# Layer B of a two-layer streaming encoder: the weight tile that was scanned for its scale is kept and split, and is not loaded a second time

## The chip, the cores and the metric

The kernel runs on one core of a Trainium2 chip. The metric is the time of one execution on the device, in microseconds (us). Runs are single executions; the median of several stands for a kernel. One further execution is recorded by the hardware profiler, and everything that is read from a trace comes from that one.

The engines are named as the profile does: PE (TensorE matmuls) with PEld (its weight loads), DVE (VectorE), ACT (ScalarE), POOL (GpSimd), SP (SyncE, which issues all DMAs here, in order).

## What is computed

Two attention layers over 2048 prompt tokens and 64 sample tokens, model width 1024, 16 heads of 64, in chunks of 64 frames. Each layer is

```
h = rms_norm(x, g);  q, k, v, gate = split(h @ w_in)
q, k = rms_norm per head;  o = softmax(q k' / 8 + bias) v
y = x + (o * silu(gate)) @ w_out
```

Layer A has 2 key/value heads, a learned sink per head and a T5 bias over the own chunk and 2 earlier ones. Layer B, where the change lies, has 16 key/value heads and a clipped relative bias over the own chunk and 8 earlier ones. The sample tokens attend to a cache (128 rows in layer A, 256 in layer B) and to themselves. The outputs are y for both, the newest keys and values of the prompt, and the rolled caches. Inputs and outputs are float32.

## The kernel before

**Precision.** Every large product is made from two parts of each operand, a high and a low one. In layer B the parts are float16, so weights have to be brought into its range: for each of the eight head pairs (hp) the kernel finds the largest absolute weight, times the norm's gain, and takes a power of two from it. `scan` (172) does this: it loads one of eight 128x512 pieces of the pair's input weights, and DVE reduces it to one maximum per partition (175). After eight pieces, `input_top` (231) takes the gain in and the maximum over the pieces; `input_across` (236) turns the column with a PE transpose (207) and works out the power of two with some ten tiny DVE passes; `input_scales` (243) spreads three numbers over all partitions with a PE matmul (222) and scales the gains (227).

**Splitting.** `load_weights` (454) loads the same pieces again for use, into a ring of 12 tiles called `wl` (470), and `split` makes the float16 parts: ACT the high one (498), DVE the low one (501). They go into another ring of 12, `wh`; eight belong to the pair in work, so at most four can be made early. `emit` (517) loads the first three pieces and queues splits; each split loads the next piece.

**Order of the work.** PE's order is written by hand. `Filler` (923) holds a list of projection jobs, one for each head pair and unit of tokens: u0 to u6, the sample unit (64 tokens), u7, then the next pair. PE alternates between attention of one unit (`pipeline`, 1717) and pieces of the projection jobs, which run about two units ahead. When a job starts, `step` (933) loads the next job's activations and, where a job a few places ahead opens a new head pair, calls its `weights` early: before, two jobs ahead with four splits (`early` = 2), and at one job ahead with the rest. The splits go into `Background` (389), a queue with costs, from which `share` (446) takes a few after each score block; in layer B at most one weight split each time. Work taken from it is ordered behind the last score pass on its engine (`anchor`, 407, and `behind`, 300), without a wait between engines. The other engines' order is made by a scheduler that moves an instruction forward where its operands are ready by its own estimate of times.

**The scans' places.** `scale_work(hp, u, e)` (271) runs after each projected tile (unit u, half e; at = 2u + e). Before, it loads one piece of the next pair's weights at each of at = 0 to 7, into the ring `wraw` of three tiles (or `scan`, of one), reduces it two tiles later, takes the maximum at at = 9, and appends `input_across` at 10 and `input_scales` at 12 to a list, `chain`. The attention loop runs one entry of that list after the fourth head of a unit (1775). Pieces 64 to 83, scanned at at = 11 to 13, belong to the output weights and the cached values.

**Attention in layer B.** `queries` (1406) transposes q and k of a unit, and ACT copies the high parts (1431, 1432); DVE makes the low ones (1443, 1447); two small DMAs copy q to the other half of the partitions (1436). At unit 1 it also loads the cache of the pair, `load_cache` (881), whose keys go into `KSA` and `KSB` (869, 870). `scores` (1459) runs the matmuls (1492, 1493; 1478 for the sample) into one of two PSUM banks `sb`; DVE adds the bias and takes the row's minimum (1496, 1501), ACT exponentiates (1505) and casts (1544), POOL subtracts for the low part (1545), a transposing DMA turns both (1553), and PE multiplies with the values (1650). For the sample, `sample_outputs` (1604) adds two parts on DVE (1614) and multiplies with the gate on POOL (1615); `sample_turned` (1617) transposes the result on PE (900).

Of the kernel before, what the change touches and what calls it, by code (L numbers as in the profile page):

```python
# [17 lines left out]
P = 128  # L18
# [10 lines left out]
HD = 64  # L29
# [24 lines left out]
TURNED = (0, 1)  # L54

@with_exitstack
def hybrid_encoder_kernel(
# [105 lines left out]
    scanned, pending = [], []  # L163

# [7 lines left out]
    def scan(i=None, keep=0):  # L172
# [71 lines left out]
    def input_scales(h):  # L244
        everywhere(h, row[:, 20:23])

# [24 lines left out]
    def scale_work(hp, u, e):  # L271
        at = 2 * u + e
        if hp < 7:
            if at < 8:
                scan(8 * (hp + 1) + at, 1)
            elif at == 8:
                scan(None, 1)
            elif at == 9:
                scan()
                input_top(hp + 1)  # L280
            elif at == 10:
                held["chain"].append(lambda: input_across(hp + 1))
            elif at == 12:
# [170 lines left out]
    def load_weights(g, *specs, scale=None):  # L454
# [7 lines left out]

        spare = 3 if len(specs) > 1 else 0
# [417 lines left out]
    def load_cache(ktsrc, vsrc, C, both):  # L881
# [41 lines left out]
    class Filler:  # L923
# [4 lines left out]
        def add(self, prefetch, weights, gen, early=3):  # L928
# [4 lines left out]
        def step(self):  # L933
            if self.gen is None:
# [35 lines left out]
    def layer_a():  # L970
# [4 lines left out]
        def add_unit(qd, place, unit):  # L975
# [120 lines left out]
            filler.add(prefetch, weights if place == 0 else None, first if qd == 0 and u == 0 else gen, 3 * (qd > 1))  # L1096
# [230 lines left out]
    def layer_b():  # L1327
# [4 lines left out]
        def add_unit(hp, unit):  # L1332
# [67 lines left out]
            filler.add(prefetch, weights if u == 0 else None, gen, 2)  # L1400
# [5 lines left out]
        def queries(it):  # L1406
# [6 lines left out]
            if u == 1:  # L1413
                load_cache(ckt_b[it.hp], cv_b[it.hp], CB, True)
# [15 lines left out]
            for hh, rows in enumerate(halves):  # L1430
                nc.scalar.activation(q1[hh][rows], qt[hh], AF.Identity, scale=gq[rows])
                nc.scalar.activation(kd[hh][rows], kt[hh], AF.Identity, scale=gk[rows])

            def copies():
                for hh, rows in enumerate(halves):
                    held["copy"] = load(wide(q1[hh][halves[1 - hh]]), wide(q1[hh][rows])).ins

# [166 lines left out]
        def sample_outputs(it):  # L1604
# [10 lines left out]
            nc.gpsimd.tensor_tensor(o, it.G[:, 0:HD], o, op=ALU.mult)  # L1615
# [399 lines left out]
```

## Time and profile before

| | |
|---|---|
| median of 3 runs | 2146.34 us (2141.74 to 2146.76) |
| profiled execution, its own time | 2147.27 us |
| span of its trace | 2145.5 us, mean granted clock 0.992 |
| instructions | 40906 |
| busy: PE, DVE, ACT, POOL | 95%, 70%, 67%, 54% of the span |
| DMA traffic of the kernel's queue | 402.35 MB, 69.7% of 16 DMA engines' span |
| layer B's input weights, second load (476) | 64 transfers of 256 KB |
| the same, load for the scan (184) | 56 transfers of 256 KB (and 8 more for the first pair, into `scan`) |

How to read it: "busy" is the share of the span in which an engine had an instruction running. Matmuls overlap, so PE's busy time counts the length of each, while its pace is set by how far apart they start. A line such as "PE sb L1492 <- DVE nm L1496: 11.5, 8, 1.9" in a list of waits says that line 1492 on PE, which works on the tile `sb`, stood idle for 11.5 us in 8 waits, the longest 1.9, and that an instruction of line 1496 on DVE, which wrote `nm`, ended them. In a timeline the columns are start, duration, engine, line, operation, output and inputs, and in brackets the idle time before and what ended it.

### The profile page before, as it was taken

The page shows a single profiled execution, that of the slowest core. Times are in us where ns is not written, and L with a number is a line of the kernel's source. Part 1 is how long each engine was busy: PE and PEld are TensorE (multiplying, and loading weights), DVE is VectorE, ACT ScalarE, POOL GpSimd, SP SyncE. Part 2 cuts the span into 40 slices and gives each one's busy share as a digit, 9 for nine tenths or more (in the row PEclk, how much of TensorE's full clock was granted, in tenths as well). Part 3 has the DMA queues.
Part 4 walks back from the last instruction along what each step waited for, and adds up shares of the span by engine and source line. Part 5 has one row for each costly group of instructions (what it writes and reads, how often), then busy time and mean ns, then how long its engine had stood idle before and what let it go on. Part 6 is the DMA issues. An engine that isn't in the chain of part 4 may idle for free.

```text
span 2145.5 us, 40906 instructions
## 1 busy us (share of the span) xinstructions
PE 2046.2 (95%) x12951; PEld 1467.4 (68%) x12951; DVE 1504.9 (70%) x4049; ACT 1428.7 (67%) x3610; POOL 1148.6 (54%) x1621
## 2 busy tenths in 40 slices
PE   7999999999999999888999999999999999898999
PEld 6887788778888999555555555555555555456887
DVE  6768778767767554677777777777867778577642
ACT  6878877767777333466667676777867768577420
POOL 5555544434445445774366676666766667566000
PEclk9999999999999999999999999999999999999999
DMA  8856545756544676744478799797887979668763
GB/s 277 269 168 209 176 155 191 211 168 212 163 149 133 211 220 182 243 149 156 136 173 205 186 194 224 169 229 177 194 213 175 241 156 202 153 144 193 228 198 116
DMA packets 512120, 404.96 MB, mean 189 GB/s; under 512 B 303696, under 2 KB 449376, under 8 KB 511872
## 3 DMA queue, kind: packets, MB, share of 16 engines
q1 hardware_dynamic: 511904, 402.35, 69.7%
q8 instruction: 102, 1.67, 0.3%
q14 instruction: 114, 0.93, 0.1%
HBM read 257.59 MB, written 73.43 MB: 154 GB/s over the span
## 4 chain that ended last, share of the span: by engine, by line
PE 62%; DVE 12%; ACT 8%; DMA 6%; issue 6%; POOL 4%; SPq 1%; ACTq 0%; DVEq 0%; POOLq 0%
PE pj L711 11%; PE pj L713 10%; PE pj L712 10%; PE pj L1858 4%; PE pj L1860 4%; PE pj L1859 4%; PE o L1650 3%; PE sa L900 2%; PE sb L1492 2%; PE tp L900 2%; PE sb L1493 2%; DVE p L1496 2%; DMA xraw<-in_x_rows_dram 1%; PE sa L1198 1%; DMA q<-q 1%
## 5 line engine op out<-in xcount | busy, mean ns | idle before, releaser
L711 PE MATMUL pj<-wh,xx 128*128 128x512 f16 (+2 forms) x1648 | 641.9, 389 | 5.3 <-ACT pb L734 2.9
L713 PE MATMUL pj<-wh,xx 128*128 128x512 f16 (+2 forms) x1648 | 623.9, 379 | 1.3 <-POOL xx L596 1.3
L712 PE MATMUL pj<-wh,xx 128*128 128x512 f16 x1024 | 390.1, 381 | 1.0 <-DVE wh L501 1.0
L1545 POOL TENSOR_TENSOR values<-p,values 128x640 f16<-128x640 f32 (+2 forms) x224 | 281.7, 1260 | 182.8 <-ACT values L1544 179.5
L1505 ACT ACTIVATE p<-p,nm 128x640 f32<-128x640 f32 (+5 forms) x264 | 199.6, 756 | 221.7 <-DVE nm L1501 175.1
L1858 PE MATMUL pj<-xx,wh 128*128 128x264 f32 (+1 forms) x1024 | 289.8, 283 | 5.8 <-DVE res L1868 3.1
L1859 PE MATMUL pj<-xx,wh 128*128 128x264 f32 (+1 forms) x1024 | 287.2, 280 | 0.0
L1496 DVE CUSTOM_DVE_ANT_0 p<-sb,BT 128x640 f32<-128x640 f32 (+5 forms) x272 | 196.5, 722 | 106.5 <-PE sb L1493 102.9
L712 PE MATMUL pj<-wl,xx 128*128 128x512 f32 (+1 forms) x624 | 233.8, 375 | 2.2 <-DVE wl L501 2.2
L596 POOL TENSOR_TENSOR xx<-xraw,xx 128x528 fp32r<-128x528 f32 (+4 forms) x144 | 185.4, 1307 | 89.3 <-ACT xx L595 75.9
L811 POOL TENSOR_TENSOR f<-f,mhalf 128x4 f32<-128x4 f32 (+2 forms) x187 | 191.5, 1025 | 11.4
L1312 POOL TENSOR_TENSOR o<-gt,o 128x256 f32<-128x256 f32 (+1 forms) x132 | 104.9, 795 | 152.7 <-ACT p L1215 91.7
L713 PEld LDWEIGHTS <-xx 128*128 128x128 f16 x1024 | 100.6, 98 | 125.4 <-issue 4.3
L816 DVE TENSOR_TENSOR pa<-pa,f 128x256 f32<-128x256 f32 (+3 forms) x221 | 143.9, 652 | 57.2 <-POOL f L811 52.4
L793 POOL TENSOR_TENSOR sq<-pa 128x256 f32<-128x256 f32 (+2 forms) x187 | 114.0, 610 | 120.1 <-ACT pa L747 79.2
L1215 ACT ACTIVATE p<-p,nm 128x257 f32<-128x257 f32 (+2 forms) x272 | 134.4, 497 | 50.5 <-DVE nm L1209 43.2
L711 PEld LDWEIGHTS <-xx 128*128 128x128 f16 x1024 | 100.9, 99 | 80.4 <-issue 2.2
L712 PEld LDWEIGHTS <-xx 128*128 128x128 f16 x1024 | 100.7, 98 | 80.1 <-issue 3.3
L1544 ACT CAST values<-p 128x640 f16<-128x640 f32 (+2 forms) x224 | 147.3, 658 | 8.3 <-DMA pt<-values 3.1
L1860 PE MATMUL pj<-xx,wl 128*128 128x264 f32 x512 | 145.4, 284 | 0.6 <-DVE wl L494 0.6
L1209 DVE CUSTOM_DVE_ANT_0 p<-sa,BT,nsink 128x256 f32<-128x256 f32 (+2 forms) x272 | 117.5, 468 | 38.3 <-PE sa L900 30.7
L1860 PE MATMUL pj<-xx,wh 128*128 128x264 f16 x512 | 141.3, 276 | 1.4 <-DVE wh L491 1.4
(279 smaller groups left out, 5023.4 us busy)
## 6 DMA issues: line engine op xcount, KB each, us to landing
xx<-xsb SPq DMA_DIRECT2D x112, 512.0 KB, 4.3
xx<-xsa SPq DMA_DIRECT2D x88, 512.0 KB, 4.9
xraw<-oga SPq DMA_DIRECT2D x64, 264.0 KB, 3.7
xraw<-ogb SPq DMA_DIRECT2D x64, 264.0 KB, 3.7
xsa<-xx SPq DMA_DIRECT2D x32, 512.0 KB, 4.0
wl<-in_w_in_b_dram SPq DMA_DIRECT2D x64, 256.0 KB, 5.1
wraw<-in_w_in_b_dram SPq DMA_DIRECT2D x56, 256.0 KB, 3.6
xraw<-in_x_dram SPq DMA_DIRECT2D x40, 256.0 KB, 3.9
```

The source lines that it names most:

```text
L596: nc.gpsimd.tensor_tensor(lo, rv, wide(hi), op=ALU.subtract)
L711: nc.tensor.matmul(ps[:n, :C], xh, wh, start=k == 0, stop=False)
L712: nc.tensor.matmul(ps[:n, :C], xh, wl, start=False, stop=False)
L713: nc.tensor.matmul(ps[:n, :C], xl, wh, start=False, stop=k == KC - 1)
L811: nc.gpsimd.tensor_tensor(fv, fv, mhalf[:n, :H], op=ALU.pow)
L1496: mi = nc.vector.tensor_tensor_reduce(out=p[r, :nk], in0=S[r, o : o + nk], in1=b, op0=ALU.add, op1=ALU.min, scale=1.0, scalar=3e38, accum_ ...
L1505: ex = nc.scalar.activation(p[:n, :nk], p[:n, :nk], AF.Exp, scale=-1.0, bias=it.nm[:n, c : c + 1], accum_out=it.sm[:n, c : c + 1],)
L1544: hi = nc.scalar.copy(two[:, :, 0, :], pv)
L1545: lo = nc.gpsimd.tensor_tensor(two[:, :, 1, :], pv, two[:, :, 0, :], op=ALU.subtract)
L1858: nc.tensor.matmul(ps[:, :OT], wh, oh, start=k == 0, stop=False)
L1859: nc.tensor.matmul(ps[:, :OT], wh, ol, start=False, stop=False)
L1860: nc.tensor.matmul(ps[:, :OT], wl, oh, start=False, stop=k == KC - 1)
```

## The change

It has six parts.

1. For head pairs 1 to 7 the scanned piece is put into the ring `wl`, remembered in `held["raws"]`, and handed to `load_weights` as `loaded`, so that it isn't fetched again. The first pair is scanned during the output projection of layer A and still loads twice.
2. Two pieces are scanned after each of at = 0 to 3, with up to two left pending; the last reductions come at at = 4 and 5. The maximum and `input_across` are placed at 5, `input_scales` at 7.
3. `early` becomes a table of "jobs ahead: splits". Layer A and the output jobs keep what they had, {3: 4}; layer B has {4: 1, 3: 1, 2: 2}. The rest is still queued one job ahead.
4. `load_cache` of layer B is called after the query copies, its key casts are ordered behind the last of them on ACT (`asked`), and its low parts behind the last score pass on DVE.
5. The gate product of the sample moves from POOL to DVE.
6. An assertion checks that the scales were made before the weights are asked for.

```diff
+EARLY, EARLY_B = {3: WN - 8}, {4: 1, 3: 1, 2: 2}
...
         if i is not None:
-            raw = t("wraw", [P, 512], WB) if keep else t("scan", [P, 512], 1)
+            if 8 <= i < 64:
+                raw = t("wl", [P, 512], WN)
+                held["raws"].setdefault(i // 8, []).append(raw)
+            else:
+                raw = t("wraw", [P, 512], WB) if keep else t("scan", [P, 512], 1)
             dst = raw if i < 80 else raw.rearrange("p (e c) -> p e c", e=2)
             behind(load(dst, scan_source(i)).ins, held["last"])
...
         if hp < 7:
-            if at < 8:
-                scan(8 * (hp + 1) + at, 1)
-            elif at == 8:
+            if at < 4:
+                scan(8 * (hp + 1) + 2 * at, 2)
+                scan(8 * (hp + 1) + 2 * at + 1, 2)
+            elif at == 4:
                 scan(None, 1)
-            elif at == 9:
+            elif at == 5:
                 scan()
                 input_top(hp + 1)
-            elif at == 10:
                 held["chain"].append(lambda: input_across(hp + 1))
-            elif at == 12:
+            elif at == 7:
                 held["chain"].append(lambda: input_scales(hp + 1))
...
-    def load_weights(g, *specs, scale=None):
+    def load_weights(g, *specs, scale=None, loaded=()):
...
+        raws += [raw.rearrange("p (k c) -> p k c", k=1) for raw in loaded]
...
         if both:
-            split_to(KSA[0:64, 0:C], KSA[64:128, 0:C], raw[0:64, :C])
-            split_to(KSB[64:128, 0:C], KSB[0:64, 0:C], raw[64:128, :C])
+            for K, r in zip((KSA, KSB), halves):
+                hi, lo = split_to(K[r, 0:C], K[halves[r.start == 0], 0:C], raw[r, :C])
+                behind(hi.ins, asked.ins)
+                behind(lo.ins, bg.anchors[lo.ins.engine])
...
-                for nxt in self.jobs[self.n + 2 : self.n + 4]:
-                    if nxt.weights is not None and nxt is self.jobs[min(self.n + nxt.early, len(self.jobs) - 1)]:
-                        nxt.weights(WN - 8)
+                for ahead, nxt in enumerate(self.jobs[self.n + 2 : self.n + 5], 2):
+                    if nxt.weights is not None and ahead in nxt.early:
+                        nxt.weights(nxt.early[ahead])
...
                 if hp not in st.emit:
-                    (st.w[hp],), _, st.emit[hp] = load_weights(1, (w_in_b[hp], 512), scale=gsb[:, hp])
+                    assert hp == 0 or len(held["chained"]) == hp
+                    (st.w[hp],), _, st.emit[hp] = load_weights(
+                        1, (w_in_b[hp], 512), scale=gsb[:, hp], loaded=held["raws"].pop(hp, ())
+                    )
...
-            filler.add(prefetch, weights if u == 0 else None, gen, 2)
+            filler.add(prefetch, weights if u == 0 else None, gen, EARLY_B)
...
-            if u == 1:
-                load_cache(ckt_b[it.hp], cv_b[it.hp], CB, True)
             tp = tp_bank()
...
-                nc.scalar.activation(kd[hh][rows], kt[hh], AF.Identity, scale=gk[rows])
+                asked = nc.scalar.activation(kd[hh][rows], kt[hh], AF.Identity, scale=gk[rows])
...
+            if u == 1:
+                load_cache(ckt_b[it.hp], cv_b[it.hp], CB, True, asked)
...
-            nc.gpsimd.tensor_tensor(o, it.G[:, 0:HD], o, op=ALU.mult)
+            nc.vector.tensor_tensor(o, it.G[:, 0:HD], o, op=ALU.mult)
```

More of the change, by code (lines that the diff above doesn't have):

```diff
@@ L163, in hybrid_encoder_kernel @@
     scanned, pending = [], []
+    held["raws"], held["chained"] = {}, []
     def scan_source(i):
@@ L245, in input_scales @@
         everywhere(h, row[:, 20:23])
+        held["chained"] += [h] * (h > 0)
     def output_top():
@@ L879, in split_at, with load_cache @@
         return x[:, :c], x[:, c:]
[L881 removed]
+    def load_cache(ktsrc, vsrc, C, both, asked=None):
         st = t("res", [P, 2 * OT], 2)
@@ L926, in __init__, with add @@
             self.attending = False
-        def add(self, prefetch, weights, gen, early=3):
+        def add(self, prefetch, weights, gen, early=EARLY):
             j = Item()
@@ L1095, in add_unit @@
                 mine[0].mark += 8 * 3 * 256 / 2400
-            filler.add(prefetch, weights if place == 0 else None, first if qd == 0 and u == 0 else gen, 3 * (qd > 1))
+            filler.add(prefetch, weights if place == 0 else None, first if qd == 0 and u == 0 else gen, EARLY if qd > 1 else {})
         for qd in range(4):
```

## The prediction, made before the changed kernel ran

> **What bounds the kernel now.** I read the page first, then the busy times of chosen stretches, the waits of TensorE (PE), and last the timelines of single engines at the end of one head pair. Layer B walks through eight head pairs; the page gives the whole:
>
> ```profile
> span 2145.5 us, 40906 instructions
> PE 2046.2 (95%) x12951; PEld 1467.4 (68%) x12951; DVE 1504.9 (70%) x4049; ACT 1428.7 (67%) x3610; POOL 1148.6 (54%) x1621
> PE 62%; DVE 12%; ACT 8%; DMA 6%; issue 6%; POOL 4%; SPq 1%; ACTq 0%; DVEq 0%; POOLq 0%
> ```
>
> PE is busy 95% of the span, and the chain that ended last is mostly PE. Whether "busy" means "at its pace" shows in the starts of two neighbouring matmuls of the projection, from the timeline of PE:
>
> ```profile
> 1308.11 0.38 PE L711 MATMUL pj<-wh,xx 128*128 128x512 f16 x1
> 1308.32 0.38 PE L712 MATMUL pj<-wh,xx 128*128 128x512 f16 x1
> ```
>
> Each is 0.38 us long, yet they start 0.21 us apart: they overlap, and the starts set the pace. The change alters no large matmul, so it can only shorten gaps in this stream. How large those are, the waits of PE say, first in one period of 130 us (1200 to 1330, about one head pair), then from 1130 to 2000:
>
> ```profile
> PE sb L1492 <- DMA q<-q: 1.7, 1, 1.7
> PE sb L1492 <- DVE nm L1496: 1.4, 1, 1.4
> PE sb L1478 <- DMA QS<-QS: 1.3, 1, 1.3
> PE o L900 <- POOL o L1615: 0.6, 1, 0.6
> ...
> PE sb L1492 <- DVE nm L1496: 11.5, 8, 1.9
> PE tp L207 <- DVE KB L1447: 6.9, 1, 6.9
> PE sb L1492 <- DMA q<-q: 6.1, 4, 1.9
> PE sb L1478 <- DMA QS<-QS: 4.8, 3, 1.8
> PE o L900 <- POOL o L1615: 3.2, 5, 0.7
> ```
>
> A head pair loses 1.7 + 1.4 + 1.3 + 0.6 = 5.0 us of 130, and the five kinds together 32.5 us. That is the ceiling of what this change can win. All four of the first list stand in one place, the end of a head pair, where the sample unit is attended. A middle stretch and such an end compare so (columns: stretch, length, busy time with count of PE, PEld, DVE, ACT, POOL, then clock, DMA share, GB/s):
>
> ```profile
> 1235.00:1261.00 26.00, 26.00 (x162) 15.18 (x161) 18.48 (x58) 18.53 (x45) 18.25 (x24) 1.00 0.90 175
> 1269.00:1295.00 26.00, 24.64 (x148) 13.92 (x147) 24.00 (x56) 22.43 (x50) 20.09 (x25) 1.00 1.00 240
> ```
>
> In the middle PE never pauses and VectorE (DVE) works 18.48 of 26 us; at the end DVE works 24.00 of 26, the DMA engines all of it; the clock is 1.00 in both. **VectorE, with the DMA engines behind it, is what PE waits for there**, and this is where the change takes work away.
>
> **The change part by part.** The sum is made against the profiled execution's 2147.27 us.
>
> *Early splits.* Before, four of the eight weight splits of the next pair are queued when the projection reaches the sample unit and four at the next job, two jobs in one crowded stretch. After, two of the eight go out three and four jobs ahead, two at the sample unit and four as before. The timeline of DVE in the crowded stretch:
>
> ```profile
> 1271.36 2.55 DVE L501 SCALAR_TENSOR_TENSOR wh<-wl,gsb,wh 128x512 f16<-128x512 f32 x2 [0.27 <-ACT wh L498]
> 1283.77 0.81 DVE L1496 CUSTOM_DVE_ANT_0 p<-sb,BT 128x640 f32<-128x640 f32 x1
> 1290.35 1.96 DVE L501 SCALAR_TENSOR_TENSOR wh<-wl,gsb,wh 128x512 f16<-128x512 f32 x2
> ```
>
> Splits stand ahead of the L1496 at 1283.77, whose bank of scores PE wants at 1283: the 1.4 us wait. The pair at 1290.35 stands ahead of the score pass from which ScalarE (ACT) goes on to the sample's queries (QS). Two splits less are 2 x (1.96 / 2) = 2.0 us less in front of these, more than the 1.4. Of the 11.5 us of that wait I count six of the eight times, since the last pair has no next pair to split for: about 6 x 1.4 = 8.4. I take two thirds, 5.5 us, because DVE is also held up by GpSimd (POOL) there; bounds 0 and 8.4. Of the QS wait's 4.8 I take a third, 1.5; bounds 0 and 4.8. The two moved splits land in the middle stretch, where DVE has 26 - 18.48 = 7.5 us free: nothing, and if that cover were gone, 2 x 0.98 per pair, 13.7 us in seven pairs.
>
> *Cache load behind the queries' activations.* The scheduler now lifts the next pair's cache split to where its target comes free, into the chain that PE waits for as "q<-q" (ACT, then the queue of SyncE, SP):
>
> ```profile
> 1303.84 0.39 ACT L869 CAST KSA<-res 64x256 fp32r<-64x256 f32 x1
> 1304.26 0.40 ACT L869 CAST KSB<-res 64x256 fp32r<-64x256 f32 x1
> 1305.25 0.45 ACT L1431 ACTIVATE q<-tp,qf 64x256 f16<-64x256 f32 x1
> 1306.80 1.13 SPq L1436 DMA_DIRECT2D q<-q  x2
> ```
>
> The new order puts both casts behind the next pair's second queries, so L1431 comes 0.39 + 0.40 = 0.8 us sooner. The four q waits give 3.2, and the single 6.9 us wait for L1447, in the same chain, another 0.8: 4.0 us; bounds 0 (the DMA is late for another cause) and 6.1. The anchor is an order on ACT itself, not a wait for another engine; what queues behind the casts in their new place are the shortest score passes of a pair: nothing.
>
> *The sample's product from POOL to DVE.*
>
> ```profile
> 1328.38 0.45 DVE L1614 TENSOR_TENSOR o<-tp,o 64x64 f32<-64x64 f32 x2
> L1615 POOL TENSOR_TENSOR o<-G,o x8: 317/318/327, 1054.2 to 1988.1; 128x64 f32<-128x64 f32 x8
> 1329.28 0.30 PE L900 MATMUL o<-ident,o 128*64 128x128 f32 x1 [0.65 <-POOL o L1615]
> ```
>
> DVE is done at 1328.83 and PE starts 0.45 us later, 0.32 of it the product. The same width costs 0.45 / 2 = 0.22 on DVE, and one handover between engines falls away. I take 0.25 us for each of the five waits, 1.3 us. Upper bound 3.2. For the lower, two rows bear on two-input passes:
>
> ```profile
> L501 DVE SCALAR_TENSOR_TENSOR wh<-wl,gsb,wh x64: 723/941/1921, 793.0 to 1813.3; 128x512 f16<-128x512 f32 x64
> L1545 POOL TENSOR_TENSOR values<-p,values 128x640 f16<-128x640 f32 (+2 forms) x224 | 281.7, 1260 | 182.8 <-ACT values L1544 179.5
> ```
>
> The same L501 takes 723 to 1921 ns. If the 1.2 us between is time behind a POOL instruction (L1545 has 1.26), the product, which also reads two tiles of SBUF, can lose as much: 8 x (1.2 - 0.25) = 7.6 us lost. I stay with 0.25, since POOL pauses while the sample's output is made. The Trainium skill, "SBUF — State Buffer", section "Who interferes with whom", states the rule that speaks against this edit: a VectorE instruction with two SBUF inputs contends with a GpSimd instruction that reads SBUF, and one of them blocks for the whole of the other. The spread of L501 agrees with it; by that rule alone the edit would lose the 7.6 instead of winning 1.3.
>
> *One load instead of two.* The DMA view lists both loads:
>
> ```profile
> q1 hardware_dynamic: 511904, 402.35, 69.7%
> wl<-in_w_in_b_dram SPq DMA_DIRECT2D x64, 256.0 KB, 5.1
> wraw<-in_w_in_b_dram SPq DMA_DIRECT2D x56, 256.0 KB, 3.6
> ```
>
> 56 transfers of 256 KB, 14.7 MB of 402, go, and 56 issues in SP's queue. Nothing in the PE list waits for weights to land, so the saving is worth what the shorter queues do for q and QS: I take 1 us; bounds 0 and what those two waits have left, 3. Of the eight loads left per pair, two go out with each tile of projection for four tiles rather than one with each of eight. They use the ring of 12 that the splits free, so SP isn't held by a reduction any more; they stay behind the latest load of x as before, and a second issue ahead of a q copy delays it by 1.13 / 2 = 0.6 us at most, which the bound of the q wait covers.
>
> *Scans closer together.* Eight reductions remain per pair, at L175:
>
> ```profile
> 1304.45 0.66 DVE L175 TENSOR_REDUCE most<-wraw 128x1 f32<-128x512 f32 x1
> DMA to landing us min/median/max: 2.6/3.6/7.0
> ```
>
> Some two more of them now fall beside the sample unit and the unit behind it: 1.36 us of DVE for each of seven pairs, 9.5 us if none were covered; DVE has gaps there while PE waits for q. I charge 1.3 us in all. The scale's chain is appended in the same step as the maximum, where a tile lay between before. It still runs only at the fourth head of the attended unit, and the projection runs ahead of that:
>
> ```profile
> 1363.24 0.15 DVE L192 TENSOR_REDUCE top<-most 128x1 f32<-128x8 f32 x1
> 1369.83 0.27 PE L207 MATMUL tp<-ident,top 128*1 128x128 f32 x1
> ```
>
> 6.6 us lie between them, so I cost it at nothing; without that lead PE would wait for one reduction and two small passes, about 1.0 us per pair, 7 in all.
>
> **Sum:** 5.5 + 1.5 + 4.0 + 1.3 + 1.0 - 1.3 = 12.0 us less: 2147.3 - 12.0 = 2135.3. The median of the runs shown, 2146.34, is 0.9 us below the profiled execution, so I forecast 2134.4, that is 0.56% less.
>
> **Rivals.**
> *The waits move on (no change).* PE would come sooner to the end of the pair and wait for the next late thing: when the score wait goes, QS and q come late by what was won, since ACT's chain sets both. For it: the four waits stand within 46 us (1283.77 to 1329.28). Against it: the edits touch three links of that chain, not one. What remains is the product's 1.3 and the single 0.8, with up to 3 us either way: 2144.
>
> *The reduction blocks DVE (slower).* DVE takes its work in order, and the reductions of half the loads now come one projected tile behind their load, where two lay between. Tiles at the sample unit can follow closely, as two evacuations of ACT show:
>
> ```profile
> 1306.94 0.47 ACT L747 ACTIVATE pa<-pj,scl 128x256 f32<-128x256 f32 x1
> 1308.96 0.47 ACT L747 ACTIVATE pa<-pj,scl 128x256 f32<-128x256 f32 x1 [1.11 <-PE pj L713]
>   DVE most L175: 2.5, 1
> ```
>
> 2.0 us apart, against a landing of 3.6 in the median and 7.0 at most: a reduction placed there holds DVE up to 5.0 us, and the next score pass with it. Over seven pairs that is 35 us against 12.0 won: 2146.3 + 23 = 2169. It decides from a delay of 12.0 / 7 = 1.7 us per pair on. Against it: before, a reduction waited for its landing but once in layer B, 2.5 us (the last line above), and a scheduler with an estimate of the landing places it.
>
> *Every wait goes.* Of the 32.5 us, all but 6 for the one at L207: 2146.3 - 26.5 = 2120.
>
> **How the numbers follow.** My forecast, a gain between 7 and 20 us, gets 0.55; all waits gone 0.13; the waits that move on 0.18; the slower case 0.14. A measurement of this kernel can tell about 0.3% (6.4 us) from no change. Faster by more holds the first and the second: 0.68; within: 0.18; slower: 0.14. The range has to leave out no more than 0.2: it runs from 2119, the case without waits, to 2150, which takes in the waits that move on, and leaves out the slower case beyond its first 4 us. Each single bound lies in it: the product at its worst gives 2134.4 + 8.9 = 2143, uncovered reductions 2134.4 + 8.2 = 2143, a chain that PE waits for 2141, moved splits without cover 2148.
>
> **What would show it.** Right: the wait of L1492 for L1496 falls from 1.4 us to under 0.5 per pair; no L869 of KSA stands between the sample's exponential and L1431; the q wait falls by about 0.8; 14.7 MB fewer in the DMA view; L1615 is on DVE at about 0.2 us. Wrong: DVE's L175 with idle time that a DMA ended, new waits of PE at L207, or the same sum of waits at the end of a pair under other names.

## The result, and the profile after

The changed kernel is slower. Its median is 2169.6 us (2159.9 to 2172.8, six runs) against 2145.5 us (2141.7 to 2152.5, six runs) for the kernel before: a ratio of 1.0103 by all runs, 95% interval 1.0077 to 1.0128 (the two medians alone give 1.0112). The forecast was 2134.4 us, the range 2119 to 2150, with a gain expected; the time went the other way. The profiled execution took 2165.0 us, its span is 2163.0.

From the page of the changed kernel (span, busy times, the kernel's queue with packets, MB and share of 16 DMA engines, the chain by engine):

```profile
span 2163.0 us, 40786 instructions
PE 2053.1 (95%) x12951; PEld 1469.9 (68%) x12951; DVE 1499.2 (69%) x4057; ACT 1428.2 (66%) x3610; POOL 1141.2 (53%) x1613
q1 hardware_dynamic: 503840, 387.67, 66.5%
PE 57%; DVE 14%; ACT 8%; DMA 7%; issue 7%; POOL 6%; SPq 1%; POOLq 0%; ACTq 0%; DVEq 0%
```

The 14.7 MB are gone, as announced, and DVE, ACT and POOL do no more than before. Yet PE's part of the chain fell from 62 to 57%: it waits more. Its waits from 1130 to 2000, to be laid beside those of the prediction (lines are moved by 6 to 14: L1492 is now L1506, L1496 is L1510, L900 is L910, L207 is L213, L1615 is L1629):

```profile
PE sb L1506 <- DVE nm L1510: 18.0, 13, 3.4
PE sb L1506 <- DMA q<-q: 15.2, 6, 3.5
PE o L910 <- DVE o L1629: 5.8, 5, 2.0
PE tp L213 <- DVE KB L1461: 5.4, 1, 5.4
```

The nm wait rose from 11.5 to 18.0 us, the q wait from 6.1 to 15.2, the o wait from 3.2 to 5.8; the QS wait of 4.8 us is no longer in the list, and L213 gave 1.5. The five kinds make 44.4 us where they made 32.5: 11.9 more. The smaller kinds, not shown, gave some of it back: all waits of this window add up to 42.5 us before and 48.9 after.

Waits are not the whole loss. The timeline of PE behind one q wait, and the busy times of that stretch (after the five engines: clock, DMA share, GB/s):

```profile
1451.01 0.48 PE L1506 MATMUL sb<-KA,q 128*128 128x384 f16 x1 [3.40 <-DMA q<-q]
...
1452.03 0.63 PE L719 MATMUL pj<-wh,xx 128*128 128x512 f16 x1
1452.46 0.63 PE L720 MATMUL pj<-wh,xx 128*128 128x512 f16 x1
```

```profile
1451.00:1454.00 3.00, 2.99 (x9) 1.29 (x10) 1.10 (x4) 0.54 (x1) 0.00 (x0) 0.50 0.84 218
```

The same matmul started every 0.21 us in the prediction's rows; here it starts every 0.43 us. The granted clock is 0.50 for 3.4 us after the gap, so each such stretch takes up to another 1.7 us from PE. The whole span had 34.1 us at half clock before and 51.2 us after.

What waits and clock make together shows in the six head pairs between the starts of the first and the seventh sample unit on PE, before and then after (columns as in the stretch above):

```profile
1035.35:1821.38 786.03, 757.26 (x4551) 435.75 (x4550) 591.63 (x1622) 574.62 (x1448) 518.22 (x702) 1.00 0.83 191
1038.83:1841.67 802.84, 764.14 (x4551) 437.58 (x4550) 586.25 (x1629) 575.37 (x1447) 512.51 (x696) 0.99 0.76 175
```

The six pairs are 16.8 us longer, of the 17.5 by which the span grew. PE runs the same matmuls in both, but is busy 757.3 us before and 764.1 after, 6.9 more, and stands idle 28.8 us before and 38.7 after, 9.9 more. In these pairs there is no half clock before and 13.7 us after, in four stretches; half of that, 6.8 us, is what the busy time grew by.

The q wait has a clear history in SP's queue. Pair 2 (counted from 0), first before (sample on PE at 1301.17), then after (sample at 1308.19):

```profile
1300.78 0.38 SPq L559 DMA_DIRECT2D xx<-xsb  x1
1301.26 1.27 SPq L1553 DMA_TRANSPOSE pt<-values  x1
...
1304.17 1.35 SPq L1553 DMA_TRANSPOSE pt<-values  x1
```

```profile
1308.80 0.43 SPq L190 DMA_DIRECT2D wl<-in_w_in_b_dram  x1
1309.28 0.91 SPq L567 DMA_DIRECT2D xx<-xsb  x2
1310.29 2.73 SPq L1567 DMA_TRANSPOSE pt<-values  x1
...
1313.12 2.92 SPq L1567 DMA_TRANSPOSE pt<-values  x1
1316.13 0.56 SPq L1329 DMA_DIRECT2D ogb<-o  x1
1316.78 1.12 SPq L1447 DMA_DIRECT2D q<-q  x2
```

Before, one load of 512 KB stands ahead of two transposing DMAs ("turns" from here on); they take 1.27 and 1.35 us of SP, with 1.6 us free between them. After, a weight piece and a second xx load have moved in front, 1.25 MB in all, and the turns take 2.73 and 2.92 us, without a gap. The queries that these copies move were ready earlier:

```profile
1313.86 0.47 ACT L1442 ACTIVATE q<-tp,qf 64x256 f16<-64x256 f32 x1
```

```profile
1319.22 0.32 PE L1506 MATMUL sb<-KA,q 128*128 128x384 f16 x1 [3.27 <-DMA q<-q]
```

The last query is written at 1314.33; its copy is issued from 1316.78 on, 2.4 us later, and PE starts at 1319.22. In pairs 2 to 5 the issue of the second q copy ends 6.3 to 7.0 us behind the start of the sample's scores before, and 9.7 to 10.4 us after.

### The profile page after: what moved, and what is told of

It is laid out like the page before. It is cut to its first block, busy times and chain, and to the rows that moved or that the text cites. A ratio compares the mean times of both kernels' runs of the same rounds, so it can differ in the third digit from the quotient of the medians.

```text
span 2163.0 us, 40786 instructions
## 1 busy us (share of the span) xinstructions
PE 2053.1 (95%) x12951; PEld 1469.9 (68%) x12951; DVE 1499.2 (69%) x4057; ACT 1428.2 (66%) x3610; POOL 1141.2 (53%) x1613
## 4 chain that ended last, share of the span: by engine, by line
PE 57%; DVE 14%; ACT 8%; DMA 7%; issue 7%; POOL 6%; SPq 1%; POOLq 0%; ACTq 0%; DVEq 0%
PE pj L719 9%; PE pj L721 9%; PE pj L720 9%; PE pj L1872 5%; PE pj L1874 5%; PE pj L1873 5%; DVE p L1510 2%; PE o L1664 2%; PE sa L910 2%; PE tp L910 2%; DVE pa L824 2%; PE sb L1506 1%; DVE wh L509 1%; PE sb L1507 1%; POOL values L1559 1%
## 5 line engine op out<-in xcount | busy, mean ns | idle before, releaser
L1510 DVE CUSTOM_DVE_ANT_0 p<-sb,BT 128x640 f32<-128x640 f32 (+5 forms) x272 | 196.4, 722 | 106.7 <-PE sb L1507 102.7
L824 DVE TENSOR_TENSOR pa<-pa,f 128x256 f32<-128x256 f32 (+3 forms) x221 | 152.6, 692 | 81.2 <-POOL f L819 76.8
L819 POOL TENSOR_TENSOR f<-f,mhalf 128x4 f32<-128x4 f32 (+2 forms) x187 | 191.0, 1022 | 10.8
```

The costliest lines, as they stand in the source:

```text
L819: nc.gpsimd.tensor_tensor(fv, fv, mhalf[:n, :H], op=ALU.pow)
L824: nc.vector.tensor_tensor(sv, sv, fv.unsqueeze(2).to_broadcast([n, H, HD]), op=ALU.mult)
L1510: mi = nc.vector.tensor_tensor_reduce(out=p[r, :nk], in0=S[r, o : o + nk], in1=b, op0=ALU.add, op1=ALU.min, scale=1.0, scalar=3e38, accum_ ...
```

## The experiments

Theory 1 after this reading: the bunched scans cost the time, in three places: their loads stand ahead of the turns in SP's queue, their reductions ahead of the sample's passes on DVE, and the early splits ahead of a score pass; PE's longer gaps then halve its clock. Rivals: one of the moved parts (splits, cache casts, product) does it alone; the kept tile does it (by its ring, or by the time that a tile is held); or the waits only move.

The table gathers all runs. "q copy" is the end of the second copy's issue behind the sample's start, pairs 2 to 5; q, nm and o are PE's waits from 1130 to 2000; "half" is the time at half clock within the span. All are us, from one profiled execution each.

| run | time, median | ratio to before, 95% | q copy | q | nm | o | half |
|---|---|---|---|---|---|---|---|
| before | 2145.5 | | 6.3-7.0 | 6.1 | 11.5 | 3.2 | 34.1 |
| after | 2169.6 | 1.0103 [1.0077, 1.0128] | 9.7-10.4 | 15.2 | 18.0 | 5.8 | 51.2 |
| e1 | 2165.4 | 1.0100 [1.0064, 1.0137] | 9.7-12.6 | 17.0 | 11.7 | 8.5 | 51.2 |
| e2 | 2146.1 | 0.9994 [0.9979, 1.0010] | 8.5-8.7 | 8.7 | 11.2 | 3.5 | 38.1 |
| e3 | 2163.9 | 1.0063 [1.0042, 1.0084] | 9.8-10.8 | 17.5 | 14.1 | 4.6 | 63.1 |
| e4 | 2148.0 | 0.9991 [0.9978, 1.0004] | 6.5-7.2 | 9.0 | 11.2 | 3.5 | 37.7 |
| e5 | 2166.8 | 1.0078 [1.0052, 1.0105] | 11.6-11.8 | 21.8 | 11.2 | 3.5 | 58.0 |
| e6 | 2154.5 | 1.0027 [1.0012, 1.0041] | 7.8-7.9 | 10.3 | 16.1 | 6.5 | 44.4 |
| e7 | 2147.6 | 1.0001 [0.9985, 1.0017] | 6.4-7.0 | 1.9 | 11.2 | 3.6 | 41.0 |
| e8 | 2163.5 | 1.0079 [1.0053, 1.0106] | 7.8-8.1 | 10.3 | 18.1 | 7.1 | 52.4 |
| e9 | 2156.3 | 1.0036 [1.0023, 1.0049] | 8.4-8.6 | 15.7 | 11.2 | 4.5 | 58.0 |
| e10 | 2156.6 | 1.0035 [1.0022, 1.0048] | 7.7-8.5 | 14.2 | 9.8 | 3.6 | 54.6 |
| e11 | 2165.5 | 1.0074 [1.0059, 1.0089] | 8.3-8.5 | 15.5 | 9.3 | 6.8 | 47.8 |
| e12 | 2167.0 | 1.0081 [1.0057, 1.0106] | 9.4-11.8 | 9.6 | 16.0 | 5.0 | 48.4 |
| e13 | 2174.5 | 1.0131 [1.0108, 1.0154] | 9.6-10.0 | 16.6 | 17.1 | 8.5 | 48.3 |
| e14 | 2145.2 | 1.0000 [0.9985, 1.0014] | 8.6-9.6 | 10.1 | 11.2 | 3.6 | 47.9 |
| e15 | 2145.7 | 0.9992 [0.9980, 1.0005] | 8.5-8.8 | 7.4 | 11.2 | 3.7 | 41.0 |
| e16 | 2147.5 | 1.0002 [0.9987, 1.0017] | 8.5-8.7 | 7.3 | 11.2 | 4.5 | 42.0 |

Ratios are each to the runs of before on the same chip (e1 to e4, e5 to e8, e9 to e12, e13 to e16 each share a chip), and comparisons below go by them.

### Which part does it: e1 to e4

**e1**, the changed kernel with the early splits as before.

```diff
-EARLY, EARLY_B = {3: WN - 8}, {4: 1, 3: 1, 2: 2}
+EARLY, EARLY_B = {3: WN - 8}, {2: 4}
```

> The changed kernel with layer B's early splits as before (four at two jobs ahead). Theory 1 (loads in front of the turns): the scan loads of a pair, no longer held back by the ring of three tiles, are issued before the sample unit, the transposing DMAs behind them take 2.7 and 2.9 us of SP's queue where they took 1.3, and the q copies come 2 us late. The splits have no part in that: 2162 to 2172 us, q wait over 3 us in most pairs. Theory 2 (the splits' new places are the cause): back to 2140 to 2150 us.

The nm wait falls to 11.7 us, the value before, so the new early splits are what raised it. But the time stays, 1.0100 against 1.0103: q and o grew by 4.5 of the 6.3 us that nm gave. The splits are visible in the waits and not in the time.

**e2**, the scans and the early splits at their old places; tile kept, cache casts and product moved.

```diff
-            if at < 4:
-                scan(8 * (hp + 1) + 2 * at, 2)
-                scan(8 * (hp + 1) + 2 * at + 1, 2)
...
+            if at < 8:
+                scan(8 * (hp + 1) + at, 1)
...
```

> The changed kernel with both the scans' places and the early splits as before; the tile is still kept, the cache casts and the product stay moved. Theory 1: one load after each projected tile, so at most four of eight can stand before the sample unit: q wait 2 us or less, 2138 to 2150 us. Theory 2: the same, since its cause is undone too. Theory 3 (the cache casts or the product, not the loads): stays at 2160 or more.

The whole loss goes: 0.9994. As the early splits alone changed nothing (e1), it is the scans' places, and neither the kept tile nor the casts or the product by themselves. In its waits, QS is gone and q has grown by half of that, 2.6 us:

```profile
PE sb L1506 <- DVE nm L1510: 11.2, 8, 1.9
PE sb L1506 <- DMA q<-q: 8.7, 5, 2.4
PE tp L213 <- DVE KB L1461: 6.0, 1, 6.0
PE o L910 <- DVE o L1629: 3.5, 5, 0.7
```

**e3**, the changed kernel with the second load put back and the scans in the ring of three.

```diff
-            if 8 <= i < 64:
-                raw = t("wl", [P, 512], WN)
-                held["raws"].setdefault(i // 8, []).append(raw)
-            else:
+            if True:
                 raw = t("wraw", [P, 512], WB) if keep else t("scan", [P, 512], 1)
```

> The changed kernel, but the scanned tile goes into the ring of three and the weights are loaded a second time, as before; scans, early splits, cache casts and product stay changed. Theory 1: the ring of three holds the scan loads back until a reduction, so the transposing DMAs are not behind eight of them: 2140 to 2155 us. Theories 2 and 3: 2160 to 2175 us.

A miss for theory 1, by which the time should have fallen: it stays at 1.0063. In its SP queue the second loads took the place ahead of the turns: three pieces and one xx load, and the second turn took 3.7 to 5.0 us in pairs 2 to 5. The reductions are still bunched here, so how the loss divides between the two isn't told by this run.

**e4**, the kernel before with the cache casts behind the queries and the product on DVE.

```diff
-            nc.gpsimd.tensor_tensor(o, it.G[:, 0:HD], o, op=ALU.mult)
+            nc.vector.tensor_tensor(o, it.G[:, 0:HD], o, op=ALU.mult)
...
+                behind(hi.ins, asked.ins)
```

> The kernel before with only the cache casts behind the queries' activations and the sample's product on VectorE. Theories 1 and 2: those two win what the prediction gave them, 4 + 1.3 us, so 2138 to 2146 us. Theory 3: 2155 us or more.

0.9991 with an interval that holds 1: of the 5.3 us that the prediction gave to these two, none can be seen. The q wait rose from 6.1 to 9.0 although the casts are out of its way: in pairs 2 to 5 the last query is ready 3.9 to 4.9 us behind the sample's start where it was 4.9 to 5.6, but the second copy lands no earlier, at 9.4 to 10.0 where it was 8.8 to 9.7.

### What of the scans does it: e5 to e11

**e5**, the changed kernel's loads alone: two per tile at at = 0 to 3, while reductions, maximum, chain and early splits stand where they stood before.

```diff
+            if at == 0:
+                scan(8 * (hp + 1), 8)
+                scan(8 * (hp + 1) + 1, 8)
+            elif at == 1:
...
+            elif at < 9:
+                scan(None, len(pending) - 1)
```

> The changed kernel with the eight scan loads two per tile as changed, but reductions, maximum, chain and early splits at the places of before. Theory 1 (bulk loads in front of the turning DMAs and the q copies): the loads alone do it, so 2158 to 2172 us, q wait above 3 us, half clock after it. Theory 4 (the bunched reductions or the earlier chain hold VectorE or PE): those are back at their old places, so 2140 to 2150 us.

The loads alone give 1.0078, 0.0084 above e2: some 18 us. In the profiled executions the six pairs from the first sample to the seventh take 801.8 us against 779.6 in e2: PE stands idle 37.1 us against 23.8, about as much more as the q wait grew (21.8 against 8.7), and is busy 764.7 us against 755.7, with 20.5 us at half clock against none. Pair 2 in its SP queue, and PE:

```profile
1306.16 0.92 SPq L190 DMA_DIRECT2D wl<-in_w_in_b_dram  x2
1307.12 0.90 SPq L574 DMA_DIRECT2D xx<-xsb  x2
1308.13 2.27 SPq L1574 DMA_TRANSPOSE pt<-values  x1
...
1310.71 5.30 SPq L1574 DMA_TRANSPOSE pt<-values  x1
```

```profile
1319.11 0.48 PE L1513 MATMUL sb<-KA,q 128*128 128x384 f16 x1 [5.28 <-DMA q<-q]
```

1.5 MB ahead, and the second turn holds SP for 5.30 us; nm and o are as in e2. Put in order of the bytes issued just ahead of the turns, the second turn of pairs 2 to 5 took 1.3 to 1.7 us behind 0.5 MB (before), 2.0 to 2.3 behind 1.0 MB (e2), 2.9 to 3.7 behind 1.25 MB (after; in e3, with 1.25 MB too, 3.7 to 5.0), 4.9 to 5.3 behind 1.5 MB (e5; in e1, with 1.5 MB too, 3.2 to 6.1). The bytes alone don't set it: the first turn of the same pairs, with the same loads ahead, took 1.3 to 2.7 us in after, e1 and e5.

**e6** (everything one unit later, the loads ordered behind the latest q copies, early splits {3: 2, 2: 2}), **e7** (e2 with three extra transfers of 256 KB, meant to stand ahead of the turns) and **e8** (the changed kernel with its loads ordered behind the latest q copies):

```diff
-            behind(load(dst, scan_source(i)).ins, held["last"])
+            behind(load(dst, scan_source(i)).ins, held.get("copy", held["last"]) if 8 <= i < 64 else held["last"])
```

> The changed kernel with the scans one unit later (two per tile after the third to sixth tile), their loads ordered behind the latest q copies in SP's queue, and the early splits as two at three jobs ahead and two at two jobs ahead. Theory 1: no scan load is left in front of the sample's copies, so the q wait falls to 2 us or less, no half clock behind it: 2128 to 2146 us. Theory 4: bunched reductions and the chain are only moved by a unit, so still 2155 or more.

> The kernel with the scans at their old places (2146 us) plus three useless transfers of 256 KB from HBM to HBM for each head pair but the first, ordered behind the latest q copies when the first tile of the pair has been projected, so in front of the sample's turning DMAs. Theory 1: the turns take 2.7 us and more of SP's queue, the q wait passes 3 us and the clock halves after it: 2158 to 2175 us. Theory 4: transfers cost nothing by themselves, 2143 to 2150 us.

> The changed kernel with nothing but the order of its scan loads changed: each stands behind the latest q copies instead of the latest load of x. Theory 1: about half of the eight then stand behind the unit after the sample, the rest right behind the sample's own copies: a time between, 2145 to 2165 us, with the q wait following the bytes that still stand in front. Theory 4: no change, 2160 to 2172 us.

e7 says nothing of the turns: the extra transfers were issued some 18 us ahead of the sample, not in front of the turns. It does show waits that move: the q wait is 1.9 us, the wait for QS 7.9, and the time as in e2. In e8 the turns are short again, 1.3 to 1.5 us, and the q wait falls from 15.2 to 10.3; but the time is 1.0079 still, with nm at 18.1 and o at 7.1. So the loads' place is not all. e6 is between, at 1.0027, a miss for theory 1, which wanted 2146 us or less and a q wait of at most 2 us.

**e9** (e5 with its loads ordered as in e8), **e10** (e2 with the same order) and **e11** (e8 with the early splits as before) take the parts singly. Their edits are those shown.

> The bunched loads stay, but behind the q copies; reductions, maximum, chain and early splits are at their old places. Theory 1 (bunched loads harm only through SP's queue, in front of the sample's two transposing DMAs, which makes the q copies late): the turns issue in 1.3 to 1.7 us each, the q wait between 1130 and 1940 falls from 21.8 us (bunched loads unpinned) to 12 or less, half clock below 48 us, time 2142 to 2151. Rival (the bunched bytes themselves, by the share of the DMA engines that they take, or the ring that they fill): the q wait stays above 16 us and the time at 2160 or more.

> The kept tile with scans and early splits at their old places, loads behind the q copies. Theory 1: it can only win what the two loads in front of the turns still cost (turns 2.1 us against 1.3, q 8.7 us in five waits): 2140 to 2146. Rival (waits move on): turns shorter, q or nm as long as before, 2146 plus or minus 2.

> The changed kernel with its loads behind the q copies and the early splits as before; only the reductions remain bunched. Theory 1 (three separate causes): the nm wait falls from 14.4 us to 8 or 9, the o wait stays at about 7 and q at about 10; time 2150 to 2159. Rival (the early splits take only what another wait would take): nm falls, but q or o rises by as much, 2162 or more. If the reductions cost nothing: 2150 or less and an o wait below 4.

e10 surprised me: the order that shortens the turns makes e2 slower, from 0.9994 to 1.0035, and its q wait goes from 8.7 to 14.2. Its SP queue and landings (DMA view of 1306 to 1320: KB each, us from issue to landing), and the same landing in the changed kernel (1308 to 1320):

```profile
1314.65 0.63 SPq L567 DMA_DIRECT2D xx<-xsb  x1
1315.38 0.47 SPq L1447 DMA_DIRECT2D q<-q  x1
1315.94 0.54 SPq L1329 DMA_DIRECT2D ogb<-o  x1
1316.57 0.47 SPq L1447 DMA_DIRECT2D q<-q  x1
1317.09 1.53 SPq L190 DMA_DIRECT2D wl<-in_w_in_b_dram  x3
...
q<-q SPq DMA_DIRECT2D x2, 32.0 KB, 3.6
```

```profile
q<-q SPq DMA_DIRECT2D x2, 32.0 KB, 2.1
```

The copies leave earlier, but 32 KB take 3.6 us to land instead of 2.1 (2.0 in e2). What differs is the load directly ahead: 512 KB of xx here, a turn and the 128 KB of `ogb` in e2 and in the changed kernel. The loads behind the copies don't account for it, since in e2 512 KB follow the copies directly as well; no run varies either side alone. The kernel before has the order of e10 and lands its copies in 3.5 us too, but they leave 0.7 to 2.2 us earlier, because its second turn starts 2.5 to 3.2 us behind the sample's start and not 3.9 to 4.6. The landing of the second copy brings these effects together. Behind the sample's start, in pairs 2 to 5, it comes at 8.8 to 9.7 us before, 9.8 to 10.3 in e2, 10.5 to 10.8 in e10, 10.7 to 11.1 in e9, 11.1 to 11.7 in the changed kernel and 12.9 to 13.2 in e5, nearly the order of their q waits. So in these rows bulk loads cost in two places: ahead of the turns by the issue, directly ahead of the copies by the landing. e9 shows the same (landing 3.5 us, q wait 15.7) and equals e10, 1.0036 against 1.0035: so that loads come in pairs costs nothing in itself; where they stand against turns and copies is what counts. My reading ahead of e9 and e10, that only the turns matter, had both times too low.

e11 keeps the reductions bunched and e9 doesn't; both have their loads behind the copies and the old early splits. 1.0074 against 1.0036 makes 0.0038 (interval about 0.0020 either way), some 8 us for the reductions, with the maximum and the scale's chain that move with them. e11 should have come out at 2150 to 2159 us by theory 1; it took 2165.5, and as its rival said, the q wait rose (15.5 against 10.3 in e8) when the nm wait fell (9.3 against 18.1). e8, with the new splits, is no slower than e11. From the first sample to the seventh, e11 takes 8.2 us more than e9: 3.5 of PE's idle time and 4.7 of its busy time, with 17.1 us at half clock against 10.2. The o wait, 6.8 against 4.5, is one place that shows the reductions. The changed kernel at the end of pair 4, DVE and then PE, and below it the kernel before, DVE in pair 3:

```profile
1602.93 1.28 DVE L177 TENSOR_REDUCE most<-wl 128x1 f32<-128x512 f32 x2
...
1605.27 0.45 DVE L1628 TENSOR_TENSOR o<-tp,o 64x64 f32<-64x64 f32 x2
...
1605.97 0.22 DVE L1629 TENSOR_TENSOR o<-G,o 128x64 f32<-128x64 f32 x1
```

```profile
1606.25 0.30 PE L910 MATMUL o<-ident,o 128*64 128x128 f32 x1 [2.01 <-DVE o L1629]
```

```profile
1457.67 0.69 DVE L175 TENSOR_REDUCE most<-wraw 128x1 f32<-128x512 f32 x1
...
1458.99 0.45 DVE L1614 TENSOR_TENSOR o<-tp,o 64x64 f32<-64x64 f32 x2
```

Two reductions of 0.64 us stand ahead of the sample's additions where one stood, and PE waits 2.01 us, the longest of the five, instead of the 0.65 of the prediction's row.

### The clock, the product, and the gain that was expected: e12 to e16

**e12**, the changed kernel with eight added matmuls ahead of the scores behind the sample, whose results are overwritten; they fill 1.9 us of the q wait.

```diff
+                if u == 7 and i == 0 and h == 0:
+                    for x in range(8):
+                        nc.tensor.matmul(S[:, 0:512], K[:, x % 2 * P : x % 2 * P + P], K[:, 0:512], start=True, stop=True)
```

> The changed kernel with eight added matmuls of 128x512 in float16, whose results are overwritten at once, on PE ahead of the first score block of the unit behind the sample, where PE waits for the q copies. They take some 1.7 us of the wait and use nothing that is late. Theory 1 (a gap of about 3 us and more on PE is followed by half clock for 3.4 us, 1.7 us more): the stretches of half clock behind the sample go, half-clock time falls from 52 us to 46 or less, and the kernel becomes 3 to 7 us faster than the changed one, 2162 to 2167 against its 2169.6, though it does more. Rival (the clock falls for another cause, or half clock costs nothing): half-clock time stays, and the time stays within 2 us or rises by up to 8 x 1.7 = 14 us where the wait is no cover.

```profile
1447.26 1.89 PE L1501 MATMUL sb<-KA 128*128 128x512 f16 x8
1452.32 0.32 PE L1509 MATMUL sb<-KA,q 128*128 128x384 f16 x1 [3.17 <-DMA q<-q]
...
1453.09 0.63 PE L719 MATMUL pj<-wh,xx 128*128 128x512 f16 x1
1453.52 0.63 PE L720 MATMUL pj<-wh,xx 128*128 128x512 f16 x1
```

Of three half-clock stretches that followed the q wait in the changed kernel (pairs 3, 4, 5), two are gone, those whose gap fell to 2.4 us and less between matmul starts; the third kept a gap of 3.55 us and stayed. But others came, in places that the edit doesn't touch, the sum is 48.4 us against 51.2, above the 46 of the expectation, and the time cannot be told from that of the changed kernel. The filling cost more than it saved: from the first sample to the seventh, 13.7 us at half clock became 6.8 and PE's idle time fell from 38.7 to 32.1 us, but the added matmuls themselves take 6 x 1.89 = 11.3 us. So that gaps bring half clock is shown by the place; no run takes half clock away at no other cost.

**e13**, the changed kernel with the product back on POOL (`nc.gpsimd` for `nc.vector` in that line).

> The changed kernel with the sample's product back on POOL. Theory 1 (the product stands behind bunched reductions on DVE): the wait of PE for it falls from 5.8 us in five waits, the longest 2.0, to 3.5 or less, the longest below 0.9, and the time by 2 to 5 us, 2164 to 2168. Rival (the wait moves on, or POOL is late as well): the o wait stays above 5 us or q or nm rises by as much, 2169 plus or minus 2.

It went the other way: the o wait rose to 8.5 us and the ratio to 1.0131 (the intervals of the two overlap). The product on DVE is not what harms; by the rows above, the additions ahead of it are late by the reductions, whoever multiplies.

**e14** (e2, but pair 1 scanned and loaded twice as before), **e15** (the kernel before with nothing but the kept tile, for pairs 2 to 7) and **e16** (the same for pairs 1 to 7):

```diff
+            if 16 <= i < 64:
+                raw = t("wl", [P, 512], WN)
+                held["raws"].setdefault(i // 8, []).append(raw)
```

> The kernel with the scans and early splits at their old places and the tile kept, but pair 1 scanned into the small ring and loaded twice as before; pairs 2 to 7 keep their tile. Theory 1 (the tile kept for pair 1 costs some 4 us at the start of layer B, and the pairs win 6.5): the first sample comes at 1034 to 1036, the wait of L824's tile near 896 goes, the six periods stay at 779 to 781, time 2139 to 2143. Rival (the later first sample has another cause, or the gain goes with it): first sample at 1039 or periods at 784 and more, 2145 to 2147.

> The kernel before with the tile kept for pairs 2 to 7 alone: no other edit of the change. Theory 1 (the kept tile is what shortens the periods; cache casts and product add nothing): six periods at 777 to 781, first sample at 1034 to 1036, time 2137 to 2143. Rival (the prediction's 1 us for it is right and the casts or the product made the shorter periods): periods at 784 to 787, 2144 to 2147.

> The kernel before with the tile kept for pairs 1 to 7: no other edit of the change. Theory 1: periods at 777 to 781 as without pair 1, first sample some 4 us later, 1038 to 1041, time 2142 to 2147, 3 to 5 us above the run without pair 1. Rival (the start of layer B differs by the schedule's chance, not by pair 1's tile): first sample at 1036 or less, or the same time as without pair 1.

All three are within 0.001 of 1. Theory 1 of this group fell: the first sample came at 1042.7, 1037.1 and 1035.5, without regard to pair 1's tile, and the six periods from sample to sample were 784.2, 781.5 and 783.1 us against 786.0 before; a single execution differs from another by as much. Kept tiles, 14.7 MB fewer, are worth nothing that can be measured here, and cost nothing either. No version beat the kernel before.

## Why the prediction was wrong, point by point

- **The step that failed** is in the paragraph on one load instead of two: "they stay behind the latest load of x as before, and a second issue ahead of a q copy delays it by 1.13 / 2 = 0.6 us at most, which the bound of the q wait covers". The price of a bulk load in SP's queue was taken as its own issue. Its price was that of the turns behind it: 1.27 and 1.35 us before, 2.73 and 2.92 after, 2.27 and 5.30 in e5. In pairs 2 to 5 the second copy landed about 2 us later for it, at 11.1 to 11.7 us behind the sample's start where it was 8.8 to 9.7, against the 0.6 us that were allowed. The trace of before held a warning: its seventh sample, with three pieces of other weights ahead of the turns, has turns of 1.9 and 2.5 us. The loads' place alone was worth about 18 us (e5 against e2), by the later landing of the q copies and by the half clock behind the longer gaps.
- **Reductions closer together** were charged with 1.3 us, bound 9.5. Measured in e11 against e9, with the earlier maximum and chain: about 8 us. The mechanism, DVE in the crowded stretch, was right, the size near its bound; the cover that I named ("DVE has gaps there while PE waits for q") doesn't hold for the sample's additions, which PE waits for behind the q wait.
- **Early splits**, 5.5 us won, were to take the wait ahead of the sample unit from 1.4 us to under 0.5 in each pair. The reading behind it was short: in the trace of before a split does end at 1281.33, but between it and the pass at 1283.77 DVE works through the low parts of queries and keys (L1443, L1447, from 1281.56 on), so a split is only the first part of what stands ahead. The changed kernel, PE and DVE in pair 2:

```profile
1276.78 0.32 PE L1506 MATMUL sb<-KA,q 128*128 128x384 f16 x1 [1.42 <-DVE nm L1510]
1292.64 0.32 PE L1506 MATMUL sb<-KA,q 128*128 128x384 f16 x1 [0.74 <-DVE nm L1510]
```

```profile
1275.18 0.49 DVE L1461 SCALAR_TENSOR_TENSOR KB<-tp,kf,KB 64x256 f16<-64x256 f32 x1
...
1275.91 0.81 DVE L1510 CUSTOM_DVE_ANT_0 p<-sb,BT 128x640 f32<-128x640 f32 x1
...
1291.10 0.74 DVE L509 SCALAR_TENSOR_TENSOR wh<-wl,gsb,wh 128x512 f16<-128x512 f32 x1
1291.76 0.82 DVE L1510 CUSTOM_DVE_ANT_0 p<-sb,BT 128x640 f32<-128x640 f32 x1
```

  The wait at the old place (1292.64, 15.6 us ahead of the sample) did fall, to 0.74 us: half of what was expected, as one split still stands ahead of the score pass. But 16 us earlier a new one of 1.42 us came up, in each of pairs 2 to 5, behind the same low parts and with no split directly ahead, and in pair 1 the old wait grew from 1.12 to 3.38 us; with the old splits (e1) neither is there. How the moved splits bring it about isn't settled. The time didn't feel any of it (e1 against the changed kernel, e8 against e11).
- **Cache casts**, 4.0 us: the order came as drawn, no KSA cast between the sample's exponential and the query's activation. L213's wait fell from 6.9 to 5.4 or 6.0, but q did not fall even in e4: it is bound by SP and by the landing, not by ACT. The chain was read one link short.
- **The product**, 1.3 us: L1629 takes 219 to 356 ns, so the estimate of 0.22 held:

```profile
L1629 DVE TENSOR_TENSOR o<-G,o x8: 219/221/356, 1057.2 to 2006.4; 128x64 f32<-128x64 f32 x8
```

  The rule of the Trainium skill, "SBUF — State Buffer", section "Who interferes with whom", by which this pass could be blocked for a whole POOL instruction, is hardly put to the test by these eight: during six of them POOL ran nothing, and the pass of 356 ns is one of the two beside a POOL instruction. So the prediction's reason for staying with 0.25, that POOL pauses there, held.
- **One load instead of two**, 1 us: nothing measurable (e15, e16).
- **The rivals.** The slower case named 2169 us, and 2169.6 came, but by another road; that the numbers meet is luck. It wanted DVE held by a landing; DVE's idle time ahead of L177 that a weight load ended is 2.2 us, once, against 2.5 before. The place, bunched scans beside the sample unit, was right and the engine wrong: SP first, DVE by its work and not by its waiting. "The waits move on" is what every neutral run shows (e2, e4, e7): where the QS wait's 4.8 us went, q took half of it (e2), and where the q wait went, QS took it (e7). This is a second step that failed: the sum added up waits as if each were time. It gave the casts, the product and the kept tile 6.3 us, that is 0.9971; with all three in place and the scans where they were (e2) the ratio is 0.9994, and its interval leaves 0.9971 out.
- **Left out** was the clock. A rule of the Trainium skill, "TensorE: Matmul & The Clock Gate", section "Part 1: The HAM clock gate (the "warmup" mystery)", says that after an idle window of some 3.4 us PE runs at half clock for about as long. The rows above agree, 0.50 for 3.4 us behind a gap of 3.40, and the trace of before shows it at its longest wait. But shorter gaps brought it too, the shortest 2.34 us between matmul starts, and here the measurement decides. I had read the clock only in stretches where it was 1.00.

What stays open: why a turn's issue grows with the bytes ahead of it (only the order in the rows is shown), how the loss splits in the changed kernel itself, where the parts overlap (18 and 8 us measured apart make more than its 22 to 24), and what the time would be without half clock.

## What to carry to other kernels

A load in an in-order queue is priced by what stands behind it: list the small, late transfers that PE waits for, and look what a bulk load directly ahead of them does to their issue and landing. Work that is to end sooner must be counted against what else the same stretch holds: the sample unit was a bad place to bring more loads and reductions to. And one wait shortened in a chain of late things can be taken up by the next, as in e2 and e7; the 14.7 MB saved here, where no wait was for these bytes, were worth nothing that can be measured.

## What the runs showed of the hardware

- The issue of a transposing DMA is no fixed cost on SP: the second of the two behind a sample (pairs 2 to 5) took 1.3 to 1.7 us behind 0.5 MB of loads (before), 2.0 to 2.3 behind 1.0 MB (e2), 2.9 to 5.0 behind 1.25 MB (after, e3) and 3.2 to 6.1 behind 1.5 MB (e1, e5). Bytes are not all of it: in e4 and e7, behind 0.5 MB, it took 1.3 to 2.3.
- A copy of 32 KB landed in 2.0 to 2.1 us where a turn and 128 KB were issued directly ahead of it (e2, after), and in 3.5 to 3.6 us where a load of 512 KB was (before, e9, e10).
- Half clock on PE came behind none of 126 gaps of 1.7 to 2.2 us between matmul starts, behind 27 of 83 from 2.2 to 3.8 us, and behind all 36 longer ones (all eighteen traces, first to last sample of layer B); the shortest was 2.34 us. It lasted 3.4 or 6.8 us, once 10.2 (e16).
